# A hybrid decoder layer on one Trainium2 core: the last quarter of the down projection kept feature-major, and the second half of the up projection's operands set at another pace

## The chip, the cores and the metric

The kernel runs on one core of a Trainium2 chip, in one launch. Five engines work side by side, each on its own list of instructions: TensorE (PE) multiplies matrices into PSUM banks, VectorE (DVE), ScalarE (ACT) and GpSimd (POOL) work element by element, and SyncE (SP) issues most DMAs. They wait for one another by semaphores. The metric is the device time of one execution in microseconds, the median of several runs; lower is better.

## The reference, cut to what matters

One layer of a decoder for 1024 prompt tokens and 8 single-token requests (1032 tokens together), model width 1024, hidden width 2816. Ahead of the part below, two parallel mixers and an output projection produce `x`.

```python
h = rmsnorm(x, w['norm2_w'])
gate, val = jnp.split(h @ w['w_up'], 2, axis=-1)
gate, buf_f_new = causal_dwconv(gate, buf_f, w['ffn_conv_w'], w['ffn_conv_b'])
x = x + (jax.nn.silu(gate) * val) @ w['w_down']
...
y = rmsnorm(x, final_norm_w)
```

## The kernel before, in words

**Products.** Every float32 operand is split into a high and a low part (ACT casts the high one, DVE subtracts it from the original), and a product is three matmuls: high by high, low by high, high by low. The residual `x` is kept feature-major: 8 tiles of 128 features by 1032 tokens.

**Up projection.** Each of 22 steps `j` takes 128 gate columns and 128 value columns of `w_up`. The 1024 inputs are cut in two halves of features, the 1032 tokens in four quarters of 258; the products are arranged so that seven of them, `p1` to `p7`, take the place of eight. Each product has 12 matmuls of 258 columns. For that, sums of weights (`up_sums`, four additions of 128x512, on POOL from `j` = 1 on) and combinations of the activations (`comb` in `set_of`, tiles `sm`) are made. `set_of(0)` makes the operands `uh`, `ul` of the first two token quarters while the output projection ends, `set_of(1)` those of the last two, on ticks that PE's matmuls give: `spread(pieces, n)` lets the next piece be written every `n` ticks. PE's list is in program order; a scheduler orders the other engines from the order in which the instructions are written and what they depend on. Step `j` = 0 does all products of the first operand set, then all of the second, in the order `FIRST`.

`final` squares each new piece of the residual on ACT (`n2sq`) and adds it on POOL (L1251) into the sum of squares; `set_norm` has PE add it over the partitions (`n2ms`, one bank each), and `rstd_of` (L736 to L739) makes the factor from it on ACT and DVE. `weigh` multiplies a residual piece by the norm's weight once its store is done. A product's result leaves its bank by an ACT copy or a DVE add (`us`, `fext`, `val`); four banks serve `ub` and `n2ms`, three serve `ua`, the residual products and, later, `dn`.

**Down projection.** The hidden activations come back from DRAM (`al`), are split (L1154) and multiplied by `w_down` in rounds of four steps (the last round has two); each product of a round, 12 matmuls of one token quarter (256, 256, 256 and 264 tokens), is added to `x1` on DVE (L1611).

**End.** In the last round (six matmuls a product) a token quarter is added (L1688), then transposed on PE to token-major blocks of 128 tokens (L1695, banks `fin`), squared and summed on ACT (L1697), scaled (DVE L1707; ACT L1704 and POOL L1705 for the other half) and stored. The quarters go in the order 3, 0, 1, 2. The last one is done otherwise: `halved` splits the residual of that quarter into high and low parts ahead of time, and `summed` adds, in two banks of 512 features for each block of 128 tokens, the products with the activations as stationary operand and the residual through identity matmuls, so that the result is token-major at once; `last_blocks` squares and scales it.

Of the kernel before, what the change touches and what calls it, by code (L numbers as in the profile page):

```python
# [16 lines left out]
P = 128  # L17
DM = 1024
# [32 lines left out]
def hybrid_layer(  # L51
# [190 lines left out]
    def after(n, work):  # L242

        later.append([n, work])
# [1073 lines left out]
    usets, combed = [{}, {}], [None]  # L1318

    def set_of(i):  # L1320
# [27 lines left out]
        def comb(out, eng, x_, y_, op):  # L1348
            t = quads(tl("x5", "sm")[:, :NT])
            out.append(t)  # L1350
            for q in range(2):
                combed[0] = eng.tensor_tensor(t[:, 2 * q:2 * q + 2], x_[q], y_[q], op=op)  # L1352
                yield
# [24 lines left out]
        else:  # L1378
            d_ = []
            yield from put("p1", a1, "hT")  # L1380
            yield from comb(d_, G, a1, b1, ALU.subtract)
# [3 lines left out]
            yield from put("p4", b2, "big")  # L1385
# [3 lines left out]
            up_sums(1, combed[0])  # L1389
# [10 lines left out]
    def up_load(j):  # L1400
        ws = []
        for c0 in (0, DFF):
            if j:
                t = wpool.tile([P, KT * P], F32, tag="ws", bufs=2, name=nm("ws"))
            else:
                t = tl("x5", "ws")[:, :KT * P]
            last_w[0] = SP.dma_start(t.rearrange("p (k m) -> p k m", m=P),
                                     w_up[0, :, c0 + j * P:c0 + (j + 1) * P].rearrange("(k p) m -> p k m", p=P))
            ws.append(t)
        wparts[j] = ws  # L1410
        if j != 1:
            up_sums(j)

    def up_sums(j, behind=None):

        (g1, g2), (v1, v2) = ((t[:, :512], t[:, 512:]) for t in wparts[j])
        sums = {}

        def add(name, x_, y_):
            sums[name] = tl("t", "wt")  # L1420
            with ExitStack() as order_:
                if behind is not None:
                    order_.enter_context(tc.issue_after(behind.ins))
                (G if j else V).tensor_tensor(sums[name], x_, y_, op=ALU.add)  # L1424
# [117 lines left out]
    with tc.manual_schedule(engines={mybir.EngineType.PE}):  # L1542
# [9 lines left out]
        after(4, lambda: spread(set_of(1), 6))  # L1552
# [72 lines left out]
    halves_ = []  # L1625

    def halved():
        identr = tl("us", "idr", F32R)[:, :P]
        A.copy(identr, ident)
        halves_.append(identr)  # L1630
        for h4 in range(2):
            hi, lo = tl("x5", "xfh", F32R)[:, :1024], tl("x5", "xfl", F32R)[:, :1024]
            halves_.append((hi, lo))
            for m in range(4):
                x_, at_ = xT[4 * h4 + m][:, quarters[2]], slice(m * 256, (m + 1) * 256)
                A.copy(hi[:, at_], x_)
                V.tensor_tensor(lo[:, at_], x_, hi[:, at_].bitcast(F32), op=ALU.subtract)
                yield

    def summed(b):  # L1640
        t0 = quarters[2].start + b * P
        tb = [bank("fin"), bank("fin")]
        for i in range(2):
            ds, first_ = slice(i * 512, (i + 1) * 512), True
            for k in range(nk):
                for a, x in ((0, 0), (1, 0), (0, 1)):
                    mm(tb[i], acts[k][a][:, t0:t0 + P], wd[k][x][:, ds], start=first_, stop=k == nk - 1 and x == 1)
                    tick()
                    if first_:
                        first_ = False  # L1650
                        for m in range(4):
                            for x_ in halves_[1 + i]:
                                mm(tb[i][:, blk[m]], x_[:, m * 256 + b * P:m * 256 + (b + 1) * P], halves_[0],
                                   start=False, stop=False)
        return t0, tb

    def last_blocks():
        for b in range(2):
            t0, tb = summed(b)
            ss = keep.tile([P, 4], F32, tag="ss", bufs=4, name=nm("fss"))  # L1660
            ot, sq = ([tl("t", "ot") for _ in range(2)] for _ in range(2))
            for i in range(2):
                ds = slice(i * 512, (i + 1) * 512)
                A.activation(sq[i], tb[i], AF.Square, accum_out=ss[:, i:i + 1])
                V.tensor_tensor(ot[i], tb[i], fw[:, ds], op=ALU.mult)
            V.tensor_tensor(ss[:, 2:3], ss[:, 0:1], ss[:, 1:2], op=ALU.add)
            A.activation(ss[:, 3:4], ss[:, 2:3], AF.Sqrt, bias=epsc, scale=1.0 / DM)
            V.reciprocal(ss[:, 3:4], ss[:, 3:4])
            for i in range(2):
                if i:  # L1670
                    A.activation(ot[i], ot[i], AF.Copy, scale=ss[:, 3:4])
                else:
                    V.tensor_scalar(ot[i], ot[i], ss[:, 3:4], None, op0=ALU.mult)
                SP.dma_start(y_prompt[0, t0:t0 + P, i * 512:(i + 1) * 512], ot[i])

    for c in (3, 0, 1, 2):
        cs = quarters[c]
        if c == 2:
            for _ in split_:
                pass  # L1680
            last_blocks()
            break
        if c == 0:
            split_ = halved()
            spread(split_, 3)
# [3 lines left out]
        for t0 in range(cs.start, cs.stop, P):  # L1689
# [11 lines left out]
            for i in range(2):  # L1701
                ds = slice(i * 512, (i + 1) * 512)
                if i:
# [36 lines left out]
```

## Time and profile before

| what | before |
|---|---|
| median of 3 runs | 1743.32 us (1743.06 to 1748.29) |
| profiled execution | 1742.79 us |
| its span | 1741.1 us |
| mean granted TensorE clock | 0.997 |
| PE busy | 1705.4 us |
| DVE, ACT, POOL busy | 1089.1, 789.8, 483.4 us |

The span runs from the first to the last instruction that the profile shows; the execution's time has a little around it. Busy times of different engines overlap. A row of the timeline gives start, duration, engine, source line, operation, output and inputs, and in square brackets the idle time of that engine just before, with what ended it. In a row of the waits stand who waited, for whom, and how long in total, how often, and the longest.

### The profile page before, as it was taken

To read this page: it belongs to the slowest core of one execution; us is meant where nothing else is said; L and a number is where in the kernel's file an instruction comes from. 1 tells how busy PE (TensorE), PEld (TensorE's weight loads), DVE (VectorE), ACT (ScalarE), POOL (GpSimd) and SP (SyncE) were. 2 spreads that over 40 slices of the span, in tenths; PEclk is the share of its full clock that TensorE was granted. 3 is DMA by queue.
4 is the path that set the end of the run, shared out by engine and by line. 5 is a ranking of instruction groups with operands and counts; after the bars stand their busy time and mean duration, and the time that the engine had idled before them with its cause. 6 is when DMAs were issued, how large, how long until landed. Compare 5 with 4: busy or idle time off the path is not lost. (4 is left out here: it accounts for less than half of the span.)

```text
span 1741.1 us, 38505 instructions
## 1 busy us (share of the span) xinstructions
PE 1705.4 (98%) x16111; PEld 1656.5 (95%) x16111; DVE 1089.1 (63%) x1983; ACT 789.8 (45%) x1441; POOL 483.4 (28%) x501
## 2 busy tenths in 40 slices
PE   7999999999999999999999989999999999999998
PEld 7999999999999999999999989999999999999997
DVE  6668666555565565567746777667676668544454
ACT  7677686344454354545334554333344334111124
POOL 2102131110120122011222266666666664000002
PEclk9999999999999999999999999999999999999999
DMA  5354334633434425335347712222222226322212
GB/s 165 73 123 120 96 91 144 186 103 105 130 94 120 115 88 142 118 99 178 119 145 252 230 53 87 97 74 74 74 80 80 97 75 240 138 90 77 86 44 98
DMA packets 250212, 200.22 MB, mean 115 GB/s; under 512 B 48020, under 2 KB 221574, under 8 KB 250022
## 3 DMA queue, kind: packets, MB, share of 16 engines
q1 hardware_dynamic: 249750, 197.67, 37.2%
q8 instruction: 126, 2.06, 0.5%
q14 instruction: 48, 0.39, 0.1%
q0 software_dynamic: 288, 0.10, 0.0%
HBM read 155.16 MB, written 46.95 MB: 116 GB/s over the span
## 5 line engine op out<-in xcount | busy, mean ns | idle before, releaser
L93 PE MATMUL mm<-hl,wh 128*128 128x344 f32 x1248 | 405.5, 325 | 0.0
L93 PE MATMUL mm<-hh,wh 128*128 128x344 f32 x1248 | 405.0, 325 | 0.0
L93 PE MATMUL mm<-hh,wl 128*128 128x344 f32 x1248 | 402.0, 322 | 0.0
L93 PEld LDWEIGHTS mm<-hl,wh 128*128 128x128 f32 x1248 | 235.4, 189 | 4.8 <-issue 4.2
L93 PEld LDWEIGHTS mm<-hh,wh 128*128 128x128 f32 x1248 | 235.4, 189 | 3.4 <-issue 2.8
L93 PEld LDWEIGHTS mm<-hh,wl 128*128 128x128 f32 x1248 | 235.6, 189 | 1.4 <-issue 1.2
L199 ACT CAST wh<-ws 128x1024 fp32r<-128x1024 f32 x96 | 100.6, 1048 | 238.8 <-PE dn L93 125.8
L93 PE MATMUL ub<-uh,wh 128*128 128x258 f32 x704 | 199.7, 284 | 4.1 <-DVE nt L737 3.3
L93 PE MATMUL ub<-uh,wl 128*128 128x258 f32 x704 | 198.9, 283 | 0.0
L93 PE MATMUL ub<-ul,wh 128*128 128x258 f32 x704 | 198.3, 282 | 0.0
L93 PE MATMUL dn<-ah,wh 128*128 128x256 f32 (+1 forms) x640 | 180.6, 282 | 1.1 <-DVE x L1611 1.1
L93 PE MATMUL dn<-al,wh 128*128 128x256 f32 (+1 forms) x640 | 180.2, 282 | 0.0
L93 PE MATMUL dn<-ah,wl 128*128 128x256 f32 (+1 forms) x640 | 179.7, 281 | 0.0
L201 DVE TENSOR_TENSOR wl<-ws,wh 128x1024 fp32r<-128x1024 f32 x88 | 115.3, 1310 | 81.0 <-ACT wh L199 81.0
L93 PE MATMUL ua<-uh,wh 128*128 128x258 f32 x528 | 149.6, 283 | 2.6 <-DVE val L1506 1.3
L93 PE MATMUL mm<-mh,wh 128*128 128x258 f32 x512 | 146.3, 286 | 4.9 <-DVE x L1233 4.1
L93 PE MATMUL ua<-uh,wl 128*128 128x258 f32 x528 | 149.3, 283 | 0.1
L93 PE MATMUL ua<-ul,wh 128*128 128x258 f32 x528 | 148.7, 282 | 0.0
L93 PE MATMUL mm<-ml,wh 128*128 128x258 f32 x512 | 145.1, 283 | 0.0
L93 PE MATMUL mm<-mh,wl 128*128 128x258 f32 x512 | 144.7, 283 | 0.0
L93 PEld LDWEIGHTS ub<-uh,wh 128*128 128x128 f32 x704 | 133.0, 189 | 4.5 <-DVE nt L737 3.5
L1444 DVE TENSOR_TENSOR wl<-wt,wh 128x512 fp32r<-128x512 f32 x88 | 89.6, 1037 | 75.1 <-ACT wh L1443 75.0
(394 smaller groups left out, 3982.5 us busy)
## 6 DMA issues: line engine op xcount, KB each, us to landing
ws<-in_w_in_dram SPq DMA_DIRECT2D x52, 512.0 KB
ws<-in_w_up_dram SPq DMA_DIRECT2D x44, 512.0 KB
ws<-in_w_out_dram SPq DMA_DIRECT2D x24, 512.0 KB
act_d<-val SPq DMA_DIRECT2D x22, 516.0 KB
al<-act_d SPq DMA_DIRECT2D x22, 516.0 KB
ws<-in_w_down_dram SPq DMA_DIRECT2D x22, 512.0 KB
ml<-mix_d SPq DMA_DIRECT2D x48, 172.0 KB
csb<-cs_d SPq DMA_DIRECT2D x32, 256.0 KB
```

What stands on the lines that cost most here:

```text
L93: PE.matmul(out, lhsT, rhs, start=start, stop=stop)
L199: A.copy(wh[:, :n], ws[:, :n])
L201: V.tensor_tensor(wl[:, :n], ws[:, :n], wh[:, :n].bitcast(F32), op=ALU.subtract)
L1444: V.tensor_tensor(lo[:, cs], sums[name], hi[:, cs].bitcast(F32), op=ALU.subtract)
```

## The change

Three parts.

1. The last quarter is done as the other three: eight products of 256 columns (six matmuls each), eight adds on DVE, sixteen transposes, squares, scaling. Only for this quarter both halves of a block are scaled on DVE. `halved`, `summed` and `last_blocks` are gone.
2. In `set_of(1)` a combination of the first halves (`comb(d_, G, a1, b1)`) stands ahead of the operand of `p1`, the operand of `p4` behind the combinations, and a piece is written every 4 ticks instead of 6.
3. The weight sums of step `j` = 1 are written together with the load of its weights, and no longer held behind the last combination.

```diff
-            yield from put("p1", a1, "hT")
             yield from comb(d_, G, a1, b1, ALU.subtract)
+            yield from put("p1", a1, "hT")
             while len(weighed) < KT:
                 yield
             yield from put("p2", a2, "big")
-            yield from put("p4", b2, "big")
             yield from comb(s_, V, b1, b2, ALU.subtract)
             yield from comb(s_, V, two(s_[0]), a1, ALU.subtract)
             yield from comb(s_, G, two(s_[1]), a2, ALU.add)
-            up_sums(1, combed[0])
+            yield from put("p4", b2, "big")
...
-        wparts[j] = ws
-        if j != 1:
-            up_sums(j)
-
-    def up_sums(j, behind=None):
-
-        (g1, g2), (v1, v2) = ((t[:, :512], t[:, 512:]) for t in wparts[j])
+        (g1, g2), (v1, v2) = ((t[:, :512], t[:, 512:]) for t in ws)
         sums = {}
 
         def add(name, x_, y_):
             sums[name] = tl("t", "wt")
-            with ExitStack() as order_:
-                if behind is not None:
-                    order_.enter_context(tc.issue_after(behind.ins))
-                (G if j else V).tensor_tensor(sums[name], x_, y_, op=ALU.add)
+            (G if j else V).tensor_tensor(sums[name], x_, y_, op=ALU.add)
             return sums[name]
...
-        after(4, lambda: spread(set_of(1), 6))
+        after(4, lambda: spread(set_of(1), 4))
...
     for c in (3, 0, 1, 2):
         cs = quarters[c]
-        if c == 2:
-            for _ in split_:
-                pass
-            last_blocks()
-            break
-        if c == 0:
-            split_ = halved()
-            spread(split_, 3)
...
-                if i:
+                if i and c != 2:
```

On POOL, at the start of the up projection, stand before: residual squares (L1251), two subtractions of the first operand set (L1479, L1480), the last combination's two pieces (L1352), then the four weight sums (L1424).

```order
L1251 TENSOR_TENSOR n2r_812<-n2r_812,n2sq_12230 128x258
L1251 TENSOR_TENSOR n2r_812<-n2r_812,n2sq_12248 128x258
L1251 TENSOR_TENSOR n2r_812<-n2r_812,n2sq_12267 128x258
L1251 TENSOR_TENSOR n2r_812<-n2r_812,n2sq_12285 128x258
L1479 TENSOR_TENSOR val_12299<-us_12398,us_12416 128x258
L1480 TENSOR_TENSOR us_12380<-us_12398,us_12380 128x258
L1352 TENSOR_TENSOR sm_12430<-sm_12405,x_1170_10444 128x516
L1352 TENSOR_TENSOR sm_12430<-sm_12405,x_1187_10581 128x516
L1424 TENSOR_TENSOR wt_12447<-ws_12423 128x512
L1424 TENSOR_TENSOR wt_12449<-wt_12447,ws_12421 128x512
L1424 TENSOR_TENSOR wt_12451<-ws_12421,ws_12423 128x512
L1424 TENSOR_TENSOR wt_12453<-wt_12449,ws_12421 128x512
```

And now (the sums are L1414, the subtractions L1469 and L1470):

```order
L1414 TENSOR_TENSOR wt_12436<-ws_12434 128x512
L1251 TENSOR_TENSOR n2r_812<-n2r_812,n2sq_12187 128x258
L1414 TENSOR_TENSOR wt_12438<-wt_12436,ws_12432 128x512
L1414 TENSOR_TENSOR wt_12440<-ws_12432,ws_12434 128x512
L1251 TENSOR_TENSOR n2r_812<-n2r_812,n2sq_12205 128x258
L1251 TENSOR_TENSOR n2r_812<-n2r_812,n2sq_12230 128x258
L1414 TENSOR_TENSOR wt_12442<-wt_12438,ws_12432 128x512
L1251 TENSOR_TENSOR n2r_812<-n2r_812,n2sq_12248 128x258
L1251 TENSOR_TENSOR n2r_812<-n2r_812,n2sq_12267 128x258
L1352 TENSOR_TENSOR sm_12387<-sm_12373,x_1170_10444 128x516
L1251 TENSOR_TENSOR n2r_812<-n2r_812,n2sq_12285 128x258
L1352 TENSOR_TENSOR sm_12387<-sm_12373,x_1187_10581 128x516
```

The four sums moved from behind the combination to between six of the residual squares, and the combination's pieces from behind the two subtractions, which now follow, to ahead of them and around the last square.

On DVE at the same place the low parts of the last operands stand before as follows (`sm_12430` is the operand of `p3`, made on POOL; L1494 frees a bank, L737 reads the norm's):

```order
L1345 TENSOR_TENSOR ul_12456<-sm_12405,uh_12455 128x1032
L1345 TENSOR_TENSOR ul_12480<-sm_12387,uh_12479 128x1032
L1478 TENSOR_TENSOR us_12416<-us_12380,ua_12400 128x258
L1345 TENSOR_TENSOR ul_12493<-sm_12329,uh_12492 128x1032
L1494 TENSOR_TENSOR fext_12298<-us_12416,ub_12341 128x258
L1506 TENSOR_TENSOR val_12299<-us_12380,ua_12425 128x258
L1345 TENSOR_TENSOR ul_12503<-sm_12430,uh_12502 128x1032
L737 SCALAR_TENSOR_TENSOR nt_12466<-n2ms_12464,n2r_812 128x258
```

And now, where POOL's combination is `sm_12387`:

```order
L1345 TENSOR_TENSOR ul_12416<-sm_12373,uh_12415 128x1032
L1345 TENSOR_TENSOR ul_12458<-sm_12387,uh_12457 128x1032
L1345 TENSOR_TENSOR ul_12424<-sm_12361,uh_12423 128x1032
L1468 TENSOR_TENSOR us_12427<-us_12380,ua_12404 128x258
L1345 TENSOR_TENSOR ul_12450<-sm_12308,uh_12449 128x1032
L1484 TENSOR_TENSOR fext_12298<-us_12427,ub_12341 128x258
L1496 TENSOR_TENSOR val_12299<-us_12380,ua_12444 128x258
L737 SCALAR_TENSOR_TENSOR nt_12478<-n2ms_12476,n2r_812 128x258
```

The split of POOL's combination moved from the last place ahead of L737 to the second of these, ahead of two other splits and three results. ACT's cast for it moved in the same way.

On DVE at the start of the down projection stand before (`x_2296` is the first output column, `x_2301` the second; `al` is the split of a stored activation, `wl` that of weights, L1525 ends the up projection's last step):

```order
L1611 TENSOR_TENSOR x_2296_18092<-x_2296_18092,dn_18094 128x256
L1525 TENSOR_TENSOR val_17817<-val_17817,fext_17816 128x1032
L1611 TENSOR_TENSOR x_2296_18092<-x_2296_18092,dn_18108 128x256
L1154 TENSOR_TENSOR al_18072<-al_18072,ah_18071 128x1032
L1611 TENSOR_TENSOR x_2296_18092<-x_2296_18092,dn_18122 128x256
L1611 TENSOR_TENSOR x_2296_18092<-x_2296_18092,dn_18136 128x264
L1611 TENSOR_TENSOR x_2301_18150<-x_2301_18150,dn_18152 128x256
L201 TENSOR_TENSOR wl_18210<-ws_18208,wh_18209 128x1024
```

And now:

```order
L1601 TENSOR_TENSOR x_2296_18092<-x_2296_18092,dn_18094 128x256
L1515 TENSOR_TENSOR val_17817<-val_17817,fext_17816 128x1032
L1154 TENSOR_TENSOR al_18072<-al_18072,ah_18071 128x1032
L1601 TENSOR_TENSOR x_2296_18092<-x_2296_18092,dn_18108 128x256
L1601 TENSOR_TENSOR x_2296_18092<-x_2296_18092,dn_18122 128x256
L1601 TENSOR_TENSOR x_2296_18092<-x_2296_18092,dn_18136 128x264
L201 TENSOR_TENSOR wl_18210<-ws_18208,wh_18209 128x1024
L1601 TENSOR_TENSOR x_2301_18150<-x_2301_18150,dn_18152 128x256
```

Each of the two splits moved ahead of one add. On PE only the last 56 matmuls changed, into 48 products and 16 transposes behind them.

More of the change, by code (lines that the diff above doesn't have):

```diff
@@ L1316, in set_norm @@
         rstd_of(rst[:, cs], tl("us", "nt"), ps[:, :QW], DM)
-    usets, combed = [{}, {}], [None]
+    usets = [{}, {}]
     def set_of(i):
@@ L1351, in comb @@
             for q in range(2):
-                combed[0] = eng.tensor_tensor(t[:, 2 * q:2 * q + 2], x_[q], y_[q], op=op)
+                eng.tensor_tensor(t[:, 2 * q:2 * q + 2], x_[q], y_[q], op=op)
                 yield
@@ L1379, in set_of @@
             d_ = []
+            yield from comb(d_, G, a1, b1, ALU.subtract)
             yield from put("p1", a1, "hT")
-            yield from comb(d_, G, a1, b1, ALU.subtract)
             while len(weighed) < KT:
@@ L1624, in hybrid_layer @@
         wd.append((hi, lo))
[L1625 to L1669, printed above, removed]
-                if i:
[L1671 to L1674, printed above, removed]
@@ L1702, in hybrid_layer @@
                 ds = slice(i * 512, (i + 1) * 512)
-                if i:
+                if i and c != 2:
                     A.activation(ot[i][:n], tb[i][:n, :], AF.Copy, scale=ss[:n, 3:4])
```

## The prediction

> **What bounds the kernel now.** I read the page's head, then TensorE's waits, the windows by stage, the chain of waits at the end, and the timelines of the two places that the change touches.
>
> ```profile
> span 1741.1 us, 38505 instructions
> PE 1705.4 (98%) x16111; PEld 1656.5 (95%) x16111; DVE 1089.1 (63%) x1983; ACT 789.8 (45%) x1441; POOL 483.4 (28%) x501
> ...
> PE ub L93 <- DVE nt L737: 3.3, 1, 3.3
> ...
> PE fin L93 <- ACT ot L1704: 1.7, 1, 1.7
> ...
> PE ua L93 <- DVE us L1478: 1.0, 1, 1.0
> ...
> 1013.49:1063.92 50.43, 44.00 (x352) 42.84 (x352) 42.16 (x64) 25.22 (x44) 29.21 (x31) 1.00 0.13 41
> 1063.92:1464.10 400.18, 400.18 (x3337) 400.18 (x3338) 275.88 (x459) 157.88 (x280) 255.06 (x253) 1.00 0.28 90
> ```
>
> TensorE is busy for 98% of the span, so time can come only from its idle places and from the work behind its last product. The windows (length, then busy time of PE, PEld, DVE, ACT, POOL) show where: from the second weight block on, the up projection has no PE idle time in 400 us, and only its first 50 us have any. The three waits and one that stands with its row below belong to the three places whose order changes: start of the up projection, start of the down projection, the last quarter. The rest keeps its order on every engine and gets zero.
>
> The profiled run took 1742.79 us around its span of 1741.1; the median is 1743.32. I predict a change of the span and add it to the median. Below 0.3%, 5.2 us here, is what a measurement of this kernel cannot tell from no change: 1738.1 to 1748.5.
>
> **The last quarter.** Each row has start, duration, engine.
>
> ```profile
> 1723.83:1725.36 1.53, 1.53 (x10) 1.38 (x11) 0.23 (x2) 1.30 (x5) 1.28 (x1) 0.95 0.41 153
> 1725.36:1728.56 3.20, 3.20 (x12) 2.71 (x11) 1.39 (x3) 1.56 (x4) 1.27 (x1) 0.50 0.47 173
> ...
> 1703.37 1.75 PE fin L1695 x16
> ...
> 1716.01 4.13 PE dn L93 x35
> ...
> 1723.83 11.02 PE fin L93 x56
> ...
> 1736.97 0.72 ACT ot L1671
> ...
> 1719.98 2.13 PE L1695 MATMUL fin<-ident,x 128*128 128x128 f32 x16
> ```
>
> Before, the sixteen transposes of the quarter ahead are issued by 1721.7 (1719.98 and 16 x 0.109, the pace of the sixteen at 1703.37), then PE waits 1.72 us for a bank and runs 56 matmuls in 11.02 us, of them 3.20 us at a granted clock of 0.50. The last store's operand is ready at 1737.69, and 3.41 us later the span ends.
>
> After, 48 products of 256 columns go to the three banks that the adds free, so the 1.72 us wait has no cause left. At 4.13/35 = 0.118 us they take 5.66: from some 1721.9 to 1727.6, plus 0.28 until the last is out. Then follow what the timeline shows for the quarter ahead:
>
> ```profile
> 1720.77 0.41 DVE L1688 TENSOR_TENSOR x<-x,dn 128x256 f32<-128x256 f32 x1
> ...
> 1724.33 0.60 ACT L1697 ACTIVATE ot<-fin 128x512 f32<-128x512 f32 x1
> ...
> 1725.83 0.75 DVE L1707 SCALAR_TENSOR_TENSOR ot<-fin,fss,fw 128x512 f32<-128x512 f32 x1
> ...
> 1715.11 1.27 POOL L1705 TENSOR_TENSOR ot<-ot,fw 8x512 f32<-8x512 f32 x1 [4.04 <-ACT ot L1704]
> 1726.59 1.27 POOL L1705 TENSOR_TENSOR ot<-ot,fw 128x512 f32<-128x512 f32 x1 [1.41 <-ACT ot L1704]
> ...
> 1718.66 0.60 ACT L1697 ACTIVATE ot<-fin 128x512 f32<-128x512 f32 x1 [1.59 <-DMA out_dram<-ot]
> ```
>
> The add, 0.41, ends at 1728.3. The transposes of its column and of the second block, 9 at that pace, end near 1729.4. From the start of a block's second square to its scaled output is 1.50 us (1724.33 to 1725.83). Block one: square 1728.6, outputs on DVE 1730.1 to 1731.5, two in a row. DVE takes block two's sum only then: sum, root and reciprocal fill the 0.9 from 1724.93 to 1725.83 above; then two outputs of 0.75, 1733.9. A buffer is the other limit: POOL's last write ends 1727.86 and its store frees the tile about 2.3 us later (1716.38, the end of the POOL row at 1715.11, to 1718.66, where ACT had waited for that store), 1730.2 for block two's second square, which gives 1733.2 and does not decide. With 3.41 us behind it the span would end at 1737.3, -3.8. Not shown is how well the four DVE outputs and the last stores pack; at the low end the half clock also returns (3.20 us at half is 1.6 lost) and 0.7 is late: -1.6; at the high end nothing waits: -4.2. I take the middle, **-2.9**. DVE's eight and ACT's nine splitting instructions that vanish lay under PE's products and are worth nothing.
>
> **The start of the down projection.** One split of a stored activation (1.22 us) is now ahead of the second add of the first output column.
>
> ```profile
> 1470.56 0.41 DVE L1611 TENSOR_TENSOR x<-x,dn 128x256 f32<-128x256 f32 x1
> ...
> 1472.03 0.41 DVE L1611 TENSOR_TENSOR x<-x,dn 128x256 f32<-128x256 f32 x1
> 1472.36 1.22 DVE L1154 TENSOR_TENSOR al<-al,ah 128x1032 fp32r<-128x1032 f32 x1
> ...
> 1471.02 0.39 PE L93 MATMUL dn<-ah,wh 128*128 128x264 f32 x1 [1.09 <-DVE x L1611]
> ```
>
> PE's three banks are full there: it waits for the add at 1470.56. The next bank is freed by the add at 1472.03; PE asks for it at 1472.57, when its 12 products from 1471.02 are issued. With the split ahead the add ends at 1472.44 + 1.15 = 1473.6: **+1.1** (0 if the other adds catch up, +1.4 with the `wl` split that also moves up).
>
> **The start of the up projection.** S is the time when POOL's last combination piece (`sm`) ends.
>
> ```profile
> 1011.00:1013.00 2.00, 2.00 (x18) 1.91 (x16) 0.69 (x1) 2.00 (x5) 0.90 (x2) 1.00 0.00 0
> 1012.31:1024.40 12.09, 11.71 (x97) 11.51 (x96) 11.65 (x19) 10.12 (x19) 3.69 (x5) 1.00 0.11 36
> ...
> 1011.91 0.64 POOL L1251 TENSOR_TENSOR n2r<-n2r,n2sq 128x258 f32<-128x258 f32 x1 [2.13 <-ACT n2sq L1250]
> ...
> 1016.30 1.16 POOL L1251 TENSOR_TENSOR n2r<-n2r,n2sq 128x258 f32<-128x258 f32 x1 [1.55 <-ACT n2sq L1250]
> ...
> 1026.07 1.61 POOL L1479 TENSOR_TENSOR val<-us,us 128x258 f32<-128x258 f32 x1 [7.55 <-issue]
> ...
> 1028.34 2.36 POOL L1352 TENSOR_TENSOR sm<-sm,x 128x516 f32<-128x516 f32 x2
> 1030.66 1.26 POOL L1424 TENSOR_TENSOR wt<-ws 128x512 f32<-128x512 f32 x1
> 1032.01 2.17 POOL L1424 TENSOR_TENSOR wt<-wt,ws 128x512 f32<-128x512 f32 x1
> ...
> 1021.08 0.69 DVE L1352 TENSOR_TENSOR sm<-sm,x 128x516 f32<-128x516 f32 x1
> ...
> 1026.99 0.42 DVE L1494 TENSOR_TENSOR fext<-us,ub 128x258 f32<-128x258 f32 x1
> 1031.82 1.23 DVE L1345 TENSOR_TENSOR ul<-sm,uh 128x1032 fp32r<-128x1032 f32 x1 [2.98 <-ACT uh L1344]
> 1032.97 0.75 DVE L737 SCALAR_TENSOR_TENSOR nt<-n2ms,n2r 128x258 f32<-128x258 f32 x2
> 1033.64 2.26 DVE L738 SCALAR_TENSOR_TENSOR nt<-nt,n2r 128x258 f32<-128x258 f32 x2
> ...
> 1030.74 1.05 ACT L1344 CAST uh<-sm 128x1032 fp32r<-128x1032 f32 x1 [5.70 <-POOL sm L1352]
> ...
> 1028.90 0.28 PE L93 MATMUL ub<-uh,wh 128*128 128x258 f32 x1
> 1033.78 0.39 PE L93 MATMUL ub<-uh,wh 128*128 128x258 f32 x1 [3.27 <-DVE nt L737]
> ```
>
> Before, POOL stands 7.55 us behind a subtraction that waits for a DVE result; S is 1030.70, ACT and DVE split that operand, and only then does DVE read the norm's bank for which PE waits. The sums come last, beside DVE's norm work.
>
> After, the four sums stand between the residual squares, as soon as their load has landed (DMA is idle from 1011 on; I take 1010.7), and the subtraction behind `sm`. POOL's row: four sums, six adds, two pieces. At the lowest prices 4 x 1.26 + 6 x 0.64 + 2.36 = 11.2, S = 1021.9, but the second piece needs DVE's of 1021.08, so S is at least 1021.77 + 1.18 = 1022.9. At the highest, 4 x 2.17 + 6 x 1.16 + 2.36 = 18.0, S = 1028.7. DVE is busy for 11.6 of the 12.1 us from 1012.31, so I take the mean of the prices plus a little: 4 x 1.72 + 6 x 0.90 + 2.36 = 14.6, 1025.3, with DVE's pieces delayed too **S = 1026.0**.
>
> The operand's split now comes ahead of two others on ACT and DVE. Behind S on DVE stand: the wait for the cast (1.05), this split and two more at 1.2 each, two adds of 0.35 as issued, so the `fext` add, which frees a bank, ends at S + 5.4 = 1031.4 (before 1027.41). PE wants that bank at 1028.90, the start of the product ahead of the one that waited; a product is 12 matmuls, 1.45 us at the windows' 0.12 each. Another 0.35 and L737's two (0.75) later, S + 6.5 = 1032.5, the norm's bank is free. PE: the first of the two products starts 1031.45, the one that waited before follows at max(1031.45 + 1.45, 1032.5) = 1032.9 instead of 1033.78: **-0.9**. The wait is not removed; it goes from the norm's bank to the `fext` add. Then the sums no longer run beside L738 (2.26 for two, where an add of the same 258 columns takes 0.42), so the 1.0 us wait for L1478 goes at least half: **-0.5**. Sum **-1.4**, between -4.5 (S = 1022.9, neither bank late: all of 3.5 and 1.0) and +1.8 (S = 1028.7, second product at S + 6.9 = 1035.6, no relief).
>
> **Sum**: -2.9 + 1.1 - 1.4 = -3.2. Span 1737.9, time **1740.1**.
>
> **Rivals.** *The sums fit.* S = 1022.9; POOL's idle time from 1018.5 on speaks for it, DVE's gapless work against. -2.9 + 1.1 - 4.5 = -6.3: 1737.0. Chance 0.24.
>
> *POOL and DVE hold each other up* (slower). Place: 1010 to 1030. The row for it is the sum that took 2.17 beside L738, 2.26 for two. All prices at the highest, and the `sm` pieces doubled too by DVE's splits: S = 1028.7 + 2.36 = 1031.1, second product at 1038.0, +4.2, no relief. -2.9 + 1.1 + 4.2 = +2.4: 1745.7; past 1748 if PE also waits for the last residual square (later than 1024.8) or the last quarter gives little. It decides from S = 1028.7, where +1.8 eats the other terms. Against it: one of the sums took 1.26 although DVE's split at 1031.82 began beside it. Chance 0.20. [...]
>
> *The half clock stays.* Something in the end stage, such as the second block's transposes or a short wait for banks, keeps PE's clock at 0.50 for 3.2 us under the 48 products: 1.6 us back, 1741.7. For it speaks that the dip follows sixteen transposes; against it that sixteen at 1703.37 left the clock alone and that the 1.72 us wait is gone. Chance 0.10. [...]
>
> **Chances and range.** Forecast 0.46, and 0.24, 0.20, 0.10. Range 1736.0 to 1747.0: the low end one below the first rival, the high end above the second. Its own range is 1737.5 to 1743. Faster by over 0.3% (under 1738.1): most of the first rival and a little of the forecast, 0.27. Slower (over 1748.5): the second rival with further delays, and several small ones together, 0.13. The rest 0.60.
>
> **What would show it.** Right: no PE wait for `ot` and no clock of 0.50 behind 1720; 48 products in 5.7 us, 6 us from the last of them to the last store's issue; a wait of about 2 us for the `fext` add at 1029 to 1031; a PE wait some 1.1 us longer at 1472. S tells the first two rivals apart: 1023, or 1031 with sums of 2 us and more. Wrong it would be if PE idles at places where no order changed, or if the last residual square holds the norm's matmul.

## The result, and the profile after

The changed kernel takes 1741.04 us (median of 20 runs, 1737.72 to 1744.07), the one before 1744.81 (20 runs, 1740.96 to 1748.29). The ratio is 0.9976, with a 95% interval of 0.9967 to 0.9984: 4.2 us less, between 2.8 and 5.8. Forecast was 3.2 less, from another median (3 runs, 1743.32). The forecast took less than 0.3% for too little to be told from no change; with 20 runs of each, 0.24% is told from none. The profiled executions differ by more, 1741.1 against 1736.0 us of span; where the rest comes from is told below.

First the head of the page after, the waits of TensorE (who waited, for whom, us in total, times, longest), and windows (length, busy time of PE, PEld, DVE, ACT, POOL, granted clock, DMA share, GB/s):

```profile
span 1736.0 us, 38515 instructions
PE 1703.0 (98%) x16119; PEld 1656.2 (95%) x16119; DVE 1087.7 (63%) x1981; ACT 785.5 (45%) x1430; POOL 484.7 (28%) x501
...
PE ub L93 <- DVE fext L1484: 2.7, 1, 2.7
...
PE dn L93 <- DVE x L1601: 2.1, 2, 1.2
...
PE ua L93 <- DVE val L1496: 0.5, 1, 0.5
...
1013.44:1031.98 18.54, 15.82 (x125) 15.27 (x125) 17.98 (x21) 12.96 (x23) 12.14 (x10) 1.00 0.07 23
1031.98:1036.47 4.49, 4.49 (x24) 4.49 (x25) 3.56 (x10) 1.14 (x2) 0.90 (x2) 0.62 0.00 0
1720.53:1726.58 6.05, 5.99 (x51) 5.79 (x49) 4.55 (x13) 3.69 (x10) 2.89 (x3) 1.00 0.52 194
```

The wait for the norm's bank (`nt`) is gone and one for the `fext` add stands in its place; the three later waits of the first two weight blocks have shrunk to one of 0.5; the down projection's start has a second bank wait; the last quarter waits for no output, at full clock. New and not forecast is the second window: behind the `fext` wait the granted clock of PE was 0.62 on average over 4.49 us.

To see where time went, three marks cut the span: the first product of the up projection, the first of the down projection, and the first transposes of the last round. Their rows before, and then after:

```profile
1013.49 0.39 PE L93 MATMUL ua<-uh,wh 128*128 128x258 f32 x1 [0.38 <-DVE x L1233]
...
1465.53 0.28 PE L93 MATMUL dn<-ah,wh 128*128 128x256 f32 x1
...
1703.21 1.91 PE L1695 MATMUL fin<-ident,x 128*128 128x128 f32 x16
```

```profile
1013.44 0.39 PE L93 MATMUL ua<-uh,wh 128*128 128x258 f32 x1 [0.93 <-DVE x L1233]
...
1463.19 0.28 PE L93 MATMUL dn<-ah,wh 128*128 128x256 f32 x1
...
1702.09 1.91 PE L1626 MATMUL fin<-ident,x 128*128 128x128 f32 x16
```

| stage (us) | before | after | change | forecast |
|---|---|---|---|---|
| up: first up to first down product | 452.04 | 449.75 | -2.3 | -1.4 |
| down: to the first transposes | 237.68 | 238.90 | +1.2 | +1.1 |
| end: to the end of the span | 37.89 | 33.91 | -4.0 | -2.9 |

The sum is -5.1, and what lies ahead of the first mark is equal here (1013.49 and 1013.44). The same three numbers of every kernel that ran carry the experiments; each is a difference of two starts in that kernel's timeline.

### The profile page after: what moved, and what is told of

Its sections match the earlier page's. It is cut to its first block, busy times and chain, and to the rows that moved or that the text cites. A ratio compares the mean times of both kernels' runs of the same rounds, so it can differ in the third digit from the quotient of the medians.

```text
span 1736.0 us, 38515 instructions
## 1 busy us (share of the span) xinstructions
PE 1703.0 (98%) x16119; PEld 1656.2 (95%) x16119; DVE 1087.7 (63%) x1981; ACT 785.5 (45%) x1430; POOL 484.7 (28%) x501
```

## The experiments

| kernel | up | down | end | time against before (95%) |
|---|---|---|---|---|
| before | 452.04 | 237.68 | 37.89 | |
| the change | 449.75 | 238.90 | 33.91 | 0.9976 (0.9967 to 0.9984) |
| e1_tail | 452.04 | 238.77 | 34.03 | 0.9985 (0.9975 to 0.9995) |
| e2_up | 449.62 | 237.71 | 35.92 | 0.9975 (0.9964 to 0.9987) |
| e3_sums | 452.49 | 237.96 | 35.93 | 0.9994 (0.9982 to 1.0006) |
| e4_set | 452.16 | 237.72 | 36.15 | 0.9990 (0.9981 to 0.9998) |
| e5_holds | 449.57 | 239.02 | 34.21 | 0.9976 (0.9966 to 0.9987) |
| e6_trans | 449.57 | 237.00 | 33.97 | 0.9967 (0.9954 to 0.9979) |
| e7_banks | 451.84 | 237.73 | 34.93 | 0.9984 (0.9973 to 0.9995) |
| e8_all | 449.65 | 236.94 | 34.05 | 0.9974 (0.9965 to 0.9983) |
| e9_less | 449.83 | 239.52 | 33.91 | 0.9976 (0.9964 to 0.9987) |
| e10_pool | 451.23 | 237.41 | 34.24 | 0.9973 (0.9960 to 0.9987) |
| e11_pace | 449.62 | 237.74 | 35.88 | one run, no interval |
| e12_three | 447.93 | 239.87 | 34.29 | 0.9962 (0.9946 to 0.9978) |

Within a stage, most kernels with the same instructions there agree to 0.4 us. One exception matters: the end of before, 37.89, where four kernels with that end have 35.88 to 36.15. Another was not followed up: the down stage of `e9_less` and `e12_three`, 0.6 and 1.0 longer than that of the change, and of `e10_pool`, 0.5 longer than that of `e8_all`. The start of the first up product is no part of the table. Nothing ahead of it was changed, yet it lies between 1013.0 and 1017.7 (the waits of `e6_trans`, for one, hold 1.5 us in which PE waited for nothing that the profile shows), so spans and ratios scatter by more than most edits are worth, and the stages are the sharper measure.

### One part alone: the end

`e1_tail` is before with the end of the changed kernel, `e2_up` before with everything else of the change.

```diff
-        if c == 2:
-            for _ in split_:
-                pass
-            last_blocks()
-            break
...
-                if i:
+                if i and c != 2:
```

> Only the last quarter is changed (feature-major products, transposes behind them); the up projection is that of before. The order of its DVE list shows that the split of a stored activation moves ahead of an add at the start of the down projection here too. Theory A (read from the two traces): the last quarter gives 3.7 us, the second bank wait at the start of the down projection costs 1.1, so -2.6 us in the span, and the up projection keeps its waits of 3.3, 1.0, 0.9 and 1.3. Rival B (the prediction's own terms): -2.9 and +1.1, -1.8 us. Rival C: the 1.6 us of the 0.50 clock depend on where the idle time falls and come back under the 48 products: -1.0 us, with a window of 3.2 us at 0.50 behind the transposes.

Measured: end 34.03, down 238.77, up 452.04 as before. The second wait at the start of the down projection is there, although the up projection and its code are the old ones: it came with the edit at the kernel's other end, since the scheduler gave the split another place once the end was written otherwise. Theory A's -2.6 is what the timed runs show (0.9985 is -2.6 us), but their interval, -4.4 to -0.9, holds rival B's -1.8 and rival C's -1.0 as well. No window of 0.50 clock lies under the products, so rival C falls. But the sum hides something that `e2_up` shows.

### One part alone: the up projection's start

```diff
+            yield from comb(d_, G, a1, b1, ALU.subtract)
             yield from put("p1", a1, "hT")
-            yield from comb(d_, G, a1, b1, ALU.subtract)
...
-            up_sums(1, combed[0])
...
-        after(4, lambda: spread(set_of(1), 6))
+        after(4, lambda: spread(set_of(1), 4))
```

> Only the up projection's start is changed (order of the second operand set, four ticks, sums with their load); the last quarter is that of before. Theory A: -2.3 us, as the difference of the two traces at the first down product; no added wait at the start of the down projection; a wait of about 2.7 us for the fext add and no waits of 1.0, 0.9 and 1.3 behind it. Rival B (the prediction's term): -1.4 us, with the waits at 1056 and 1064 still there. Rival D: the 3.2 us at clock 0.50 that follow the 2.7 us wait in the trace of after belong to that wait and come again; if they do not come, -3.8 us.

Measured: up 449.62, -2.4, and no second wait in the down projection. Its last quarter is word for word that of before, and yet it is 2 us shorter. The chain of waits shows the 56 matmuls, and the window over them the clock:

```profile
1722.01 9.41 PE fin L93 x56
...
1722.00:1726.00 4.00, 3.99 (x26) 3.60 (x27) 1.55 (x5) 2.84 (x8) 2.51 (x2) 1.00 0.45 166
1726.00:1730.00 4.00, 4.00 (x27) 3.55 (x26) 1.70 (x5) 2.01 (x5) 0.06 (x1) 1.00 0.26 96
```

Before had 11.02 for the same 56, with 3.20 us at 0.50. The 1.72 us wait for a bank stands in both. So the half clock does not come with that end each time: it stands in the profiled execution of before and in none of the other four kernels with this end (35.88 to 36.15). Against those, the new end gives 2.0 us, not 4.0. How often the timed executions of before had it is not shown, and it need not be rare: over `e1_tail`, `e2_up`, `e3_sums`, `e4_set` and `e7_banks` the timed runs differ from before by -2.6, -4.4, -1.0, -1.7 and -2.8 us; the stages add up to -2.8, -4.4, -1.2, -1.6 and -3.1 against before as profiled, and to 1.9 more each (-0.9, -2.5, +0.7, +0.3, -1.2) with the dip taken out of it. The timed executions of before are longer than its stages without the dip, by this dip or by something else. Rival D's -3.8 did not come: the clock dipped again behind the 2.7 us wait, and it mattered as little as in the changed kernel, as the next two parts show.

### Where the up projection's gain comes from

`e3_sums` moves only the sums to their load, `e4_set` only the order inside the second operand set.

```diff
-            up_sums(1, combed[0])
...
-        if j != 1:
-            up_sums(j)
+        up_sums(j)
```

> Only the four weight sums are moved to their load; the combination stays behind the two subtractions, its split just ahead of the norm. Theory A: the gain of the up projection's start comes from the sums no longer running beside the norm's work, which takes away the three later waits (1.0, 0.9, 1.3): -3 us, with the 3.3 us wait for the norm's bank still there. Rival E: it comes from the combination's earlier place, so nothing is gained here: 0 us, all four waits there.

> Only the order of the second operand set is changed, at six ticks: the combination stands ahead of the subtractions, the sums directly behind it (still not with their load), the split of the combination stays just ahead of the norm. Theory A: S near 1023 to 1025, the norm's bank free by 1031 to 1032, so the 3.3 us wait shrinks to about 1; the sums end near 1031 instead of 1037, so the later waits go too: -4 to -5 us. Rival E: the combination's place alone gives the 3.3 us back and the later waits stay: -2 to -3 us. Rival F: sums and DVE's splits share 1024 to 1031 and the wait stays: 0 to -1 us.

Both missed. `e3_sums`: up 452.49. The later waits went, as theory A had it, but the wait for the norm's bank grew from 3.3 to 4.6 and a stretch at half clock followed. `e4_set`: up 452.16. S came at 1023.57, the earliest of all kernels, and the sums behind it then stood beside DVE's splits: the `fext` add came at 1032.46, PE waited 3.7 for it and 0.6 for the norm. Rival F was nearest. Neither the place of the combination nor the place of the sums gained anything alone, in runs where the clock was at half for 6.83 us behind the long wait; what that cost is taken up below.

`e11_pace` has four ticks and the sums with their load, without the two moves inside the set:

> The kernel before with four ticks instead of six and the sums with their load, but the old order inside the second operand set and the old last quarter. The order of its DVE and POOL lists at this place is that of e2_up but for names. Theory: 449.6 from the first up to the first down product, as e2_up, so the two moves inside the set are idle. Rival: they were needed, 452.

Measured: 449.62. The pace and the sums together are the whole gain; the moves of `p1` and `p4` are idle. The pace alone was not run. Here the same wait of 2.72 us was followed by no dip, and the stage is as long as in `e2_up` with one.

### What sets the end of the start stage

What all kernels with 449.6 share, and not those with 452, is the place of one DVE instruction, the last `val` add of a weight block. Its rows for the first two blocks, before and then after:

```profile
1043.15 0.42 DVE L1506 TENSOR_TENSOR val<-us,ua 128x258 f32<-128x258 f32 x1
...
1063.45 0.41 DVE L1506 TENSOR_TENSOR val<-us,ua 128x258 f32<-128x258 f32 x1
```

```profile
1040.82 0.42 DVE L1496 TENSOR_TENSOR val<-us,ua 128x258 f32<-128x258 f32 x1
1061.12 0.41 DVE L1496 TENSOR_TENSOR val<-us,ua 128x258 f32<-128x258 f32 x1
```

Counted from the first up product, it stands at 29.66 before and at 27.38 after, 2.28 earlier, and the second 20.30 behind it in both. The up stage is shorter by 2.29. The link is a wait: PE's last stop in the stage is for that second add, before, after and in `e12_three` (below):

```profile
1063.92 0.39 PE L93 MATMUL ua<-uh,wh 128*128 128x258 f32 x1 [1.26 <-DVE val L1506]
```

```profile
1061.59 0.39 PE L93 MATMUL ua<-uh,wh 128*128 128x258 f32 x1 [0.46 <-DVE val L1496]
```

```profile
1060.37 0.39 PE L93 MATMUL ua<-uh,wh 128*128 128x258 f32 x1 [2.79 <-DVE val L1509]
```

From that product to the first down product it takes 401.4 to 401.6 us in all eleven kernels that have this wait. `e3_sums`, `e4_set` and `e10_pool` have none: there PE, at half clock for 6.83 us, came last, and DVE stood waiting for it ahead of its first `val` add:

```profile
1044.40 0.42 DVE L1476 TENSOR_TENSOR us<-us,ua 128x258 f32<-128x258 f32 x1 [1.20 <-PE ua L93]
...
1041.11 0.42 DVE L1478 TENSOR_TENSOR us<-us,ua 128x258 f32<-128x258 f32 x1 [0.60 <-PE ua L93]
...
1043.84 0.42 DVE L1476 TENSOR_TENSOR us<-us,ua 128x258 f32<-128x258 f32 x1 [0.94 <-PE ua L93]
```

So the 452.49 and 452.16 of the first two hold a cost of the half clock, and what their orders are worth without it is not shown.

`e1_tail` had a 3.3 us wait and then a window at 0.51 clock where before had none:

```profile
1034.08:1037.30 3.22, 3.22 (x15) 3.22 (x16) 3.22 (x3) 1.99 (x4) 3.22 (x3) 0.51 0.00 0
```

and yet its `val` add stands at 29.66 and its up stage is 452.04, equal to before: PE's loss was taken out of a later wait of its own (the 0.98 for `us` is gone). So PE's waits in this stage are not what the time is made of, as long as DVE's list ends later. `e5_holds` tests that with another order of the list:

```diff
+                with ExitStack() as order_:
+                    if behind is not None:
+                        order_.enter_context(tc.issue_after(mark[behind].ins))
                     V.tensor_tensor(lq[:, rows], t, hq[:, rows].bitcast(F32), op=ALU.subtract)
...
-            yield from put("p5", [s_[0]], "hT")
+            yield from put("p5", [s_[0]], "hT", "fext")
```

> The changed kernel with DVE's splits for p5 and p7 held behind the fext add that frees a bank, and the split for p3 behind the first of the norm's two instructions. Theory A (DVE's order at this place makes the 2.7 us wait, nothing else does): the fext add ends near 1028.5 instead of 1031.9, the wait for it falls below 0.5, the norm's bank is free by 1032.2, so PE waits about 1.7 there instead; the first p7 product of the second half starts 1.2 earlier, 2.8 with no stretch at 0.50: -1.2 us against the changed kernel. Rival G (DVE's whole work between 1012 and 1041 is the limit, and its order only moves the wait): later waits for us, val and the like come back, 0 us.

Measured: 449.57, no gain. The wait for `fext` is gone, the norm's bank is waited for (2.2), the clock stays at 1.00 throughout, and a 1.7 us wait for the `val` add takes up what was won. Rival G was right. DVE's list of this kernel shows why its better order did not end earlier:

```profile
1027.63 1.22 DVE L1352 TENSOR_TENSOR ul<-sm,uh 128x1032 fp32r<-128x1032 f32 x1
...
1029.57 3.33 DVE L1352 TENSOR_TENSOR ul<-sm,uh 128x1032 fp32r<-128x1032 f32 x2
```

One split alone took 1.22; two beside POOL's subtractions (0.75 and 1.74 from 1029.36 on) took 3.33, 0.9 more than twice that. DVE lost by collision what it no longer lost by waiting.

`e9_less` and `e12_three` leave work out of that list: one split, and three, of DVE's (the low part of another operand is used in their place).

```diff
+            if i and name in ("p5", "p7", "p3"):
+                usets[i][name] = hq, usets[i]["p1"][1]
+                A.copy(hq, src[0])
+                yield
+                return
```

> The kernel of e5_holds with DVE's split of the last operand (p3 of the second half, 1.22 us) left out: p3 uses the low part of p1's operand again, so its low products are not the reference's. That split stands behind the norm, and PE waited for nothing behind it until the val add of the second weight block (1.7 us). Theory G (DVE's queue over the first weight block sets the end: its last val add stood at 27.4 us behind the first up product in the changed kernel, e5 and e6 alike, 29.7 in before): that add comes at 26.2, the one of the second block 20.3 us later, and the time from the first up product to the first down product falls from 449.6 to 448.4. Rival A (PE's own waits at 1030 to 1034 set it): no change, 449.6.

Measured: 449.83; theory G's 448.4 did not come. A combination on DVE met one on POOL and took 1.69 instead of 0.68, all behind it came 1.0 later, PE's clock fell to 0.67 in the window behind, and DVE waited 0.34 for PE. The run decides nothing between the two.

> The kernel of e5_holds with three of DVE's splits left out (p5, p7 and p3 of the second half, 3.6 us; the low part of p1's operand is used again, so their low products are not the reference's). In the run with one left out the saved 1.2 us were lost to a POOL collision of 1.0 and a wait for PE at half clock, so it told nothing. Theory G (DVE's queue over the first weight block sets the end of the start stage): norm's bank free by 30.5 - 13 = 17.5 us behind the first up product, DVE's last val add of the block at 25.9 or earlier instead of 27.4, and 448.1 or less from the first up to the first down product instead of 449.6. Rival K (something that is not on DVE, PE's own products or POOL's subtractions): 449.6 as in the five kernels before.

Measured: 447.93, and the `val` add 24.27 us behind the first up product:

```profile
1030.61 0.75 DVE L739 SCALAR_TENSOR_TENSOR nt<-n2ms,n2r 128x258 f32<-128x258 f32 x2
...
1038.18 0.42 DVE L1509 TENSOR_TENSOR val<-us,ua 128x258 f32<-128x258 f32 x1
```

The first up product is at 1013.91 there. Theory G holds: less work on DVE over the first weight block shortens the stage, 1.6 us for 3.6 left out. Not all of it, since PE still waits 2.8 us for the second block's `val` add, at 1059.90: behind three fewer splits, other DVE work of the second block comes last. The down stage of this run, 0.85 longer than that of `e5_holds`, took back half of it, for a reason that no run shows.

`e10_pool` tries to use that: the split of the last operand goes from DVE to POOL, on the kernel of `e8_all`.

```diff
-                    V.tensor_tensor(lq[:, rows], t, hq[:, rows].bitcast(F32), op=ALU.subtract)
+                    (G if i and name == "p3" else V).tensor_tensor(lq[:, rows], t, hq[:, rows].bitcast(F32), op=ALU.subtract)
```

> The kernel of e8_all with that same split on POOL instead of DVE, right behind the combination that it splits. [...] Rival J (an operation with two operands in SBUF on POOL holds DVE up for about as long as it saves, as the sums did beside L738): 449.6 or more, with DVE's splits beside it at 1.7 to 2.4 instead of 1.2.

Measured: 451.23, 1.6 worse than `e8_all`, and not the 448.4 that 1.22 us less on DVE's list alone would give (449.65 less 1.22). Rival J's numbers came, and the rows of both engines show the collision:

```profile
1032.38 4.38 DVE L1352 TENSOR_TENSOR ul<-sm,uh 128x1032 fp32r<-128x1032 f32 x2
...
1031.14 2.84 POOL L1352 TENSOR_TENSOR ul<-sm,uh 128x1032 fp32r<-128x1032 f32 x1 [1.78 <-ACT uh L1348]
1033.94 1.73 POOL L1477 TENSOR_TENSOR val<-us,us 128x258 f32<-128x258 f32 x1
```

Two splits that take 2.4 alone took 4.38, and POOL's own subtraction 1.73 where it takes 0.74 later in the stage. For 1.22 saved DVE paid 1.94. Not all of the 1.6 need be the collision's: PE waited 4.0 for the norm's bank and was at half clock for 6.83 us around the end of that wait, where `e8_all` has 2.2 and 3.41, and DVE then waited 0.94 for PE. How the loss divides between collision and clock is not shown.

### The start of the down projection, and the bank of the old end

`e6_trans` holds the second round's splits behind the first columns' adds. `e8_all` has that and the holds of `e5_holds`.

```diff
-            split_in(hi, lo, slice(0, NT))
+            if not later_:
+                split_in(hi, lo, slice(0, NT))
...
+                    if r0 == 0 and 0 < m + i <= RND:
+                        with tc.issue_after(last_x.ins):
+                            split_in(*nxt[m + i - 1], slice(0, NT))
```

> The changed kernel with the splits of the second round's stored activations held behind the first columns' adds of the first round, so that at the start of the down projection no split stands ahead of an add. Theory A: the two waits for banks there (1.2 and 0.9) go, -2.1 us against the changed kernel. Rival H (the first wait belongs to the convolution's last pass ahead of the adds on DVE, which stays): only the 0.9 goes.

> The changed kernel with the holds of both other edits (splits of the second operand set behind the fext add and the norm; splits of the second round behind the first columns). Theory A: both gains add, -3.3 us against the changed kernel, -7.5 against before. Rival G: only the second, -2.1 and -6.3.

Measured: down 237.00 and 236.94, 1.9 less than the change and 0.7 less than before; neither kernel has a PE wait for an add there. Theory A holds for `e6_trans`, rival G for `e8_all`. Timed, `e6_trans` is the fastest kernel that computes everything, 0.9967 of before against 0.9976, but the intervals overlap, and `e8_all`, which has the same stages within 0.1 us, came out at 0.9974: that it beats the change is shown by the stages and not by the times.

`e7_banks` is before with the first block of the old end in the banks of the down products.

```diff
-        tb = [bank("fin"), bank("fin")]
+        tb = [bank("fin"), bank("fin")] if b else [psmm.tile([P, 512], F32, tag="mm", name=nm("fin")) for _ in range(2)]
```

> The kernel before, with the last quarter's first block in the banks of dn instead of the four that the transposes use; nothing else moves. Theory A: the 1.7 us wait for a bank goes, and the tail without a stretch at 0.50 is 1.7 us shorter than the 268.1 us that the two kernels with the same end showed from the first waiting down product to the end of the span: 266.4, against 267.2 in the changed kernel, so the feature-major end with its transposes is no better than the old one, the bank was. Against before -1.7 us, -3.3 us where before has the 0.50 stretch. Rival I: the products then wait for the block's residual or the scaled outputs wait for buffers, and the end moves by less than 0.5.

Measured: end 34.93, 1.0 less than that end without the dip and 1.0 more than the new end; 267.2 from the first waiting down product on, not theory A's 266.4, and more than rival I's 0.5. The wait for a bank is gone. Its chain of waits shows what came instead:

```profile
1728.04 2.01 DMA out_dram<-ot
...
1730.17 0.69 DVE ot L1665
...
1732.01 2.02 DMA out_dram<-ot
...
1734.15 0.69 DVE ot L1665
```

Twice DVE stands until a store has given its tile back, the mechanism of rival I. The old end's outputs and squares share four tiles, and these hold it as soon as banks no longer do.

## Why the prediction was right, and where it was right for another reason

Its time, 1740.1, lies 0.9 from the median, and the sign and the range hold. In part that is luck: with the end at full clock the stages give -2.3, +1.2 and -2.0, together -3.1 against the -3.2 forecast, since 0.9 forecast too little for the start of the up projection and 0.9 too much for the end cancel. By its own steps:

**The last quarter.** Right in mechanism: no wait for a bank, no 0.50 clock under the products, 48 products in 6.05 us where 5.66 and the gaps were forecast. The rows of the finish:

```profile
1726.78 0.42 DVE L1619 TENSOR_TENSOR x<-x,dn 128x256 f32<-128x256 f32 x1 [0.29 <-PE dn L93]
...
1729.53 1.41 DVE L1638 SCALAR_TENSOR_TENSOR ot<-fin,fss,fw 128x512 f32<-128x512 f32 x2
...
1731.62 1.41 DVE L1638 SCALAR_TENSOR_TENSOR ot<-fin,fss,fw 128x512 f32<-128x512 f32 x2
```

The last output is ready at 1733.03, 6.3 us behind the last product (6 was forecast), and the span ends 2.97 behind it. The worked sum was -3.8 and the measured difference of the two profiles -4.0; the term in the forecast, -2.9, was a middle between bounds (the lower of which is -1.5 by its own numbers, not -1.6). What it got wrong is what the bounds mean. It took the 3.20 us at 0.50 for a property of the old end, and only asked whether the new one would have it as well. The runs show that 1.9 of the 4.0 goes with a dip that one of five profiles of that end had, 1.6 of it in the 56 matmuls (11.02 against 9.41). The change of the end at full clock is -2.0.

**The start of the down projection.** +1.1 forecast (its own figures, 1473.6 less 1472.57, give 1.0), +1.2 measured, of which 1.03 is in PE's waits (2.12 against 1.09), and the mechanism in the rows, the split ahead of the add and PE's second wait:

```profile
1469.83 1.22 DVE L1154 TENSOR_TENSOR al<-al,ah 128x1032 fp32r<-128x1032 f32 x1
1470.97 1.08 DVE L1601 TENSOR_TENSOR x<-x,dn 128x256 f32<-128x256 f32 x3
...
1471.43 0.38 PE L93 MATMUL dn<-ah,wh 128*128 128x256 f32 x1 [0.90 <-DVE x L1601]
```

**The start of the up projection.** -1.4 forecast, -2.3 measured, and here the step failed. S was right, and so was the new wait:

```profile
1024.31 1.21 POOL L1352 TENSOR_TENSOR sm<-sm,x 128x516 f32<-128x516 f32 x1 [1.31 <-DVE sm L1352]
...
1026.60 3.51 DVE L1345 TENSOR_TENSOR ul<-sm,uh 128x1032 fp32r<-128x1032 f32 x3
...
1031.51 0.41 DVE L1484 TENSOR_TENSOR fext<-us,ub 128x258 f32<-128x258 f32 x1
...
1031.98 0.39 PE L93 MATMUL ub<-uh,wh 128*128 128x258 f32 x1 [2.71 <-DVE fext L1484]
```

S is 1025.52 (1026.0 forecast), the `fext` add ends at 1031.92 (1031.4), PE waits 2.7 (about 2). But the product that "starts 1032.9 instead of 1033.78: -0.9" started no earlier: in `e6_trans`, at full clock, 20.60 us behind the first up product, against 20.29 before. The gain is all in the later waits: 0.98, 0.85 and 1.26 became one of 0.46. The term for them, -0.5, priced the first alone; the 1.26 for the `val` add, longer than that and in the waits of before, was left at nothing without a reason, and it is the one that ends the stage. The failed step is to cost the stage by PE's waits one after another. What counts there is when DVE is done with the first weight block, since the second block's `val` add, for which PE waits last in eleven of the fourteen kernels, comes 20.1 to 20.3 us behind the first one's in all but `e12_three`. In the 28 us behind the first up product before, DVE was idle for 4.0 between 12 and 20; after, for 1.0. Of these 3.0, 2.3 made the `val` add earlier and 0.7 went into longer busy time. Each later wait looked small because PE reached it late from the one before.

**The rivals.** The first, sums that fit, would have had S at 1022.9 and both banks early; no kernel had that. `e4_set` had S at 1023.57, with the sums behind it, and no gain. The second was right in kind and wrong in price: POOL and DVE did hold each other up: DVE came to its add of L1460 at 1024.09 where before it was 1021.68 (L1470), and the two splits behind it took 2.25 instead of 1.30. These 3.4 are more than the 2.6 that the sums had cost beside the norm, where L738 and L739 now take 0.76 for two instead of 2.26 and 1.85: collisions cost DVE more than before, and the idle time that went outweighs it. The row that was named against this rival, a sum of 1.26 beside the split at 1031.82, ends at 1031.92 and says little. `e10_pool` shows the same in kind: where the two engines' operations met, both took longer, DVE's two splits 1.9 more than alone, beside POOL operations of 2.84 and 1.73, the second of which took 0.74 later in the stage. By what mechanism is not shown. The third, half clock under the 48 products, came in none of the eight kernels with the new end.

## What to carry to other kernels

- Where a wait of the bound engine moves from one place to the next, cost the list of the engine it waits for up to the last thing needed in that stage, and not the waits one by one; a list with collisions and idle time in it says more than the sum of the waits.
- A stretch at half clock in one profiled execution need not be in the next (the one at the end of before stood in one of five with that end): look for it in a second profile of the same code before it is put into a sum as a gain, and hold the sum of the stages against the timed runs.
- An edit at one end of a scheduled program can move instructions at the other; compare the order of every engine's list over the whole program, and test each part alone.

## What the runs showed of the hardware

In these profiles the granted clock fell to 0.50 behind some PE waits of 1.7 to 4.6 us, for 3.41 us or for twice that (6.83 in `e3_sums`, `e4_set`, `e7_banks` and `e10_pool`), and not behind others of the same length in the same code. At the start of the up projection, a wait of 3.27 us left it at 1.00 before; 3.33 in `e1_tail` and 3.30 in `e7_banks`, the same instructions, were followed by the dip. Behind 2.71 in the change and 2.72 in `e2_up` it dipped, behind 2.73 in `e6_trans` and 2.72 in `e11_pace` not; behind 2.21 in `e8_all` it dipped, behind 2.22 in `e5_holds` not.

In the traces of before and of the change the dips keep to a grid. The first windows of 0.02 us at 0.50 start at 315.52, 1725.22 and 1738.88 in before and at 315.62, 1032.42 and 1732.16 in the change. The first two of each trace lasted 3.41 us; the third runs to the end of the span. The starts in a trace lie, within 0.02 us, 413 and 4, and 210 and 205 times 3.4133 us apart. With stretches of that length counted from there, the 3.27 us wait of before is cut in two; the 2.71 us wait of the change lies in one, and the next is at half clock. First before, then after (length, then busy time of PE; the clock is 1.00 or 0.50):

```profile
1028.91:1032.32 3.41, 1.59 (x14) 1.39 (x12) 0.50 (x1) 1.58 (x3) 3.33 (x4) 1.00 0.00 0
1032.32:1035.73 3.41, 1.95 (x16) 1.95 (x17) 3.41 (x5) 1.70 (x5) 3.41 (x3) 1.00 0.00 0
```

```profile
1029.01:1032.42 3.41, 0.70 (x6) 0.48 (x5) 2.91 (x4) 2.43 (x6) 1.81 (x2) 1.00 0.00 0
1032.42:1035.83 3.41, 3.41 (x18) 3.41 (x17) 2.92 (x9) 1.14 (x2) 0.46 (x1) 0.50 0.00 0
```

In the stretch ahead of the dip PE was idle for 2.71 us in the change, though it was busy for 0.70. Counted back by 3.41 from the dip of each kernel, its matmul rows give some 3.0 in `e1_tail`, 2.4 in `e7_banks`, 2.3 in `e2_up`, 2.2 in `e9_less` and 2.0 in `e10_pool`. The two stretches of before above, which no dip followed, have 1.82 and 1.46. One pair does not fit: the dip under the last products of before followed a stretch with 1.72 idle (1721.81 to 1725.22), and in `e2_up` a stretch with nothing but transposes and the wait of 1.72 (1718.60 to 1722.01) brought none. A second stretch at half clock followed where PE was idle in the first for some 0.9 (`e7_banks`) and 2.0 (`e10_pool`), and not at 0.4 (`e2_up`), 0.3 (`e1_tail`) and 0.00 (the change). That the place of a wait in the grid decides is the author's reading of these numbers; no run was made for it. The sixteen transposes of 1703.21 in before and 1702.09 in the change, without a wait behind them, brought no dip: from 1702 to 1710 the clock is 1.00 in both.

Open remains what decides after `e12_three`: which of DVE's instructions of the second block its 2.8 us wait comes from was not tried. Open too is what makes the timed executions of before longer than its stages at full clock.
